# Compression's product in two parts, and the attention gate's projections ahead of the recurrent steps, in a decoder trunk of two layers

## The chip, the cores and the metric

The kernel runs on one core of one Trainium2 chip. The metric is the device time of one execution in microseconds. A core has five engines with a queue each, and each works through its own instructions in the order in which they stand: TensorE (PE, with its weight loads as PEld), VectorE (DVE), ScalarE (ACT), GpSimd (POOL) and SyncE (SP). Engines wait for each other, and for transfers, by semaphores. In this kernel SyncE and ScalarE issue all the transfers.

## What is computed

Two layers over a sequence of 1024 tokens of width 1024. Each layer normalises, projects with one wide matrix, and splits the result among four mixers: attention in three branches, a gated MLP, a convolution module and an RWKV-7 recurrence. Each mixer's output is multiplied by its own gate, an output projection and a residual follow, then a gated per-layer embedding. The parts that matter here:

```python
def nsa_compress(k, pos, w1, w2):
    ch = k.reshape(B, S // CMP_STRIDE, CMP_STRIDE, dk)
    blk = jnp.concatenate([ch[:, :-1], ch[:, 1:]], axis=2) + pos
    flat = blk.reshape(B, -1, CMP_BLOCK * dk)
    return jax.nn.silu(flat @ w1) @ w2          # w1: (2048, 128), once for keys, once for values

# conv module:  x = a * sigmoid(b); causal depthwise convolution of 31 taps; ...
# RWKV-7:
def step(state, inp):
    sa = jnp.einsum('bhvk,bhk->bhv', state, -kk_t)
    state = state * w_t + sa * (kk_t * a_t) + v_t * k_t
    return state, jnp.einsum('bhvk,bhk->bhv', state, r_t)

# layer: mix = concat(y_a * silu(z_a), y_b * silu(z_b), y_c * silu(z_c), y_d * silu(z_d))
```

## The kernel before, in words

The work is cut into four halves: half 0 and half 1 are the two halves of the sequence (512 tokens each) in the first layer, halves 2 and 3 the same in the second. For each half the string in `ORDER` names the steps in the order in which they are written: H norm, F the recurrence's front, R its chain (`rwkv_chain`, which calls `rwkv_solve`), N the attention's front (`nsa_front`), r the recurrent steps (`rwkv_steps`), G the convolution's GLU, a, b, c, d the four gates' projections (`zgate`), s the gated MLP, n the recurrence's norm, A a tile of attention, T the convolution's taps, C its end, O and g the output products of the half before, and so on. That order is a priority, not the final order: the framework's scheduler decides at build time, from priority and its own idea of how long things take, where each engine's instructions stand. On the chip these orders are fixed.

Activations lie with channels on partitions and tokens along the row. Every dense product is made in three passes of 128x512 (`mm3`, L168 to L170: high times high, low part of the activations, low part of the weights). Weights come in granules of 128x512: a load into `ws` (L152), a cast to the high part `wh` on ScalarE (L158), a difference that gives the low part `wl` on GpSimd (L160), and in the first half of each layer a store of the low part to DRAM (L163, `low`), from which the second half loads it (L157). `ws`, `wh` and `wl` have three buffers each. A projection of 128 columns is 24 dense products and two granules.

The recurrence is done in chunks of 64 tokens. Its chain makes, for all chunks and heads, the inverse of a unit triangular matrix: TensorE makes the matrices (L444, L447), VectorE masks them (L465), SyncE stores them to DRAM (`Nd`, L459, L466) and loads them back with one matrix to a partition (L471 into `q`, L476 into `l`). VectorE then solves row by row, 15 rounds of a product and a sum (L484, L486) and 16 more (L506, L508), a long series in which each round needs the one before. The result goes to DRAM from ScalarE's queue (`Xd`, L496), and the steps load it back on SyncE's (`x`, L536). In `rwkv_tri` TensorE's first product with it is L540, VectorE masks that (L543), the second product is L547, and VectorE adds (L550). The steps themselves are L588 to L626 on TensorE with VectorE, ScalarE and GpSimd in between (L596, L601, L608, L621), eight chunks one behind the other. L647 and L648 belong to the norm behind them.

The compression's product (L871) multiplies patches of the keys and values (`im`, made on VectorE at L856) with `nsa_w1`, whose eight parts of 128x512 are loaded on SyncE into the pool `ld` (`load_w1`, L831). The pool has five buffers. So five parts (four of the keys', one of the values') are loaded at the start of `nsa_front`, and the other three when the product itself has let go of a buffer. The product stands at the end of `nsa_front`, behind the key, value and query projections, and is followed by four short steps to the compressed keys and values (L874 to L902).

The convolution's GLU (L679 on VectorE) stands behind two projections; as soon as it is there, VectorE can start on the 31 taps for each of two groups of channels (L691, then 30 of L694, 60 in a half), which have no hurry. A gate's projections end in L658 on ScalarE and L659 on VectorE.

## Time and profile before

| | us |
|---|---|
| median of three runs | 1815.43 |
| lowest and highest of the three | 1801.3, 1817.22 |
| the profiled execution, its own time | 1803.61 |
| its span, first to last instruction | 1801.9 |

| engine | busy us | share of the span | instructions |
|---|---|---|---|
| PE | 1676.2 | 93% | 10068 |
| DVE | 1207.2 | 67% | 3217 |
| ACT | 798.9 | 44% | 1801 |
| POOL | 400.1 | 22% | 327 |

A busy engine is not yet the bound: the share is a mean over stretches with different limits. What to read is which wait ends last in a stretch. In the rows below, a number in brackets behind an instruction is the time in which its engine stood idle before it, with what ended that. The granted clock of TensorE is given as a share of its full level (1.00 is 2.4 GHz, 0.50 is 1.2 GHz); over the whole span it was 0.966.

### The profile page before, as it was taken

How to read it: one execution, taken by the hardware profiler on the slowest of the kernel's cores; microseconds unless marked ns; L12 is line 12 of the kernel's file. 1: busy time of each engine (PE TensorE's matmuls, PEld its weight loads, DVE VectorE, ACT ScalarE, POOL GpSimd, SP SyncE). 2: the span in 40 equal slices, each digit the busy share in tenths (PEclk: the TensorE clock that was granted, in tenths of full speed). 3: DMA queues.
4: the chain of work that ended last, by engine and by line, in shares of the span. 5: the costliest groups of instructions: out<-in, count | busy, mean ns of one | idle time of the engine just before them, and what ended most of it. 6: DMA issues, size and time to landing. Idle time of an engine off the chain costs nothing. (4 is left out here: it accounts for less than half of the span.)

```text
span 1801.9 us, 29197 instructions
## 1 busy us (share of the span) xinstructions
PE 1676.2 (93%) x10068; PEld 1237.6 (69%) x10068; DVE 1207.2 (67%) x3217; ACT 798.9 (44%) x1801; POOL 400.1 (22%) x327
## 2 busy tenths in 40 slices
PE   5997999999999999989988999999999999998998
PEld 4665666767776766666666667666777777766777
DVE  5649887765988647566499961667578885464263
ACT  4432244653234655544322434556333446553443
POOL 3333233000011232233332323000000102323343
PEclk9999998999999999989989999999999999989989
DMA  8466553326844523464574455753475433114554
GB/s 270 135 158 151 163 164 114 108 83 156 226 137 118 164 94 122 154 184 127 148 177 144 127 183 172 235 172 104 124 195 157 120 106 106 42 53 146 170 164 123
DMA packets 361419, 261.19 MB, mean 145 GB/s; under 512 B 84652, under 2 KB 296624, under 8 KB 361272
## 3 DMA queue, kind: packets, MB, share of 16 engines
q1 hardware_dynamic: 318520, 245.17, 46.8%
q10 hardware_dynamic: 42752, 14.16, 3.1%
q8 instruction: 79, 1.29, 0.3%
q14 instruction: 68, 0.56, 0.1%
HBM read 191.50 MB, written 67.77 MB: 144 GB/s over the span
## 5 line engine op out<-in xcount | busy, mean ns | idle before, releaser
L168 PE MATMUL mm<-aT,wh 128*128 128x512 f32 (+1 forms) x1304 | 537.4, 414 | 7.6 <-ACT aT L257 2.8
L169 PE MATMUL mm<-aT,wh 128*128 128x512 f32 (+1 forms) x1304 | 531.0, 408 | 3.3 <-DVE aT L258 3.1
L170 PE MATMUL mm<-aT,wl 128*128 128x512 f32 (+1 forms) x1304 | 529.0, 406 | 0.2 <-POOL wl L160 0.2
L160 POOL TENSOR_TENSOR wl<-ws,wh 128x512 fp32r<-128x512 f32 (+1 forms) x228 | 307.3, 1350 | 697.2 <-ACT wh L158 593.5
L158 ACT CAST wh<-ws 128x512 fp32r<-128x512 f32 (+2 forms) x388 | 237.1, 611 | 477.7 <-PE mm L169 297.4
L168 PEld LDWEIGHTS mm<-aT,wh 128*128 128x128 f32 (+1 forms) x1304 | 249.6, 192 | 68.5 <-issue 6.2
L169 PEld LDWEIGHTS mm<-aT,wh 128*128 128x128 f32 (+1 forms) x1304 | 249.1, 191 | 58.1 <-DVE aT L258 7.4
L170 PEld LDWEIGHTS mm<-aT,wl 128*128 128x128 f32 (+1 forms) x1304 | 249.2, 191 | 51.6 <-issue 3.3
L694 DVE SCALAR_TENSOR_TENSOR cv<-cv,cw,cv 128x512 f32<-128x512 f32 x240 | 198.2, 843 | 2.3
L973 ACT COPY pt<-pt 128x512 f32<-128x512 f32 (+1 forms) x152 | 80.6, 530 | 110.8 <-PE pt L970 110.1
L608 POOL TENSOR_TENSOR q<-SB,gc 128x256 f32<-128x256 f32 x28 | 23.0, 821 | 474.6 <-DVE SB L621 178.7
L1032 ACT ACTIVATE r<-s,sma 128x512 f32<-128x512 f32 (+3 forms) x192 | 105.8, 554 | 46.4 <-DVE sma L1030 42.9
L970 PE MATMUL pt<-cst,r 128*128 128x128 f32 x528 | 103.2, 294 | 9.5 <-DVE r L1037 9.2
L978 PEld LDWEIGHTS pv<-pt,vs 128*64 128x64 f32 x1056 | 56.4, 138 | 58.4 <-ACT pt L973 48.5
L978 PE MATMUL pv<-pt,vs 128*64 128x128 f32 x1056 | 94.4, 291 | 2.2 <-ACT pt L973 1.8
L970 PEld LDWEIGHTS pt<-cst,r 128*128 128x128 f32 x528 | 60.9, 143 | 45.9 <-issue 24.7
L1022 DVE CUSTOM_DVE_ANT_0 s<-s,T 128x256 f32<-128x256 f32 (+1 forms) x144 | 54.0, 378 | 42.8 <-PE s L1003 42.1
L1002 PE MATMUL s<-kv,qs 128*128 128x512 f32 (+2 forms) x192 | 74.3, 389 | 0.8 <-ACT r L1032 0.8
L1037 DVE TENSOR_SCALAR r<-r,sma 128x640 f32<-128x640 f32 (+7 forms) x128 | 67.4, 526 | 1.0
L1003 PE MATMUL s<-kv,qs 128*128 128x512 f32 (+2 forms) x192 | 65.7, 346 | 0.0
L1034 DVE TENSOR_TENSOR sma<-sma 128x1 f32<-128x1 f32 x64 | 14.1, 220 | 71.2 <-ACT r L1032 70.9
L1113 DVE SCALAR_TENSOR_TENSOR ot<-ot,ld 128x512 f32<-128x512 f32 x24 | 25.1, 1049 | 51.3 <-ACT ot L1112 49.4
(328 smaller groups left out, 2652.7 us busy)
## 6 DMA issues: line engine op xcount, KB each, us to landing
ws<-in_w_in_dram SPq DMA_DIRECT2D x232, 256.0 KB, 3.2
wl<-low SPq DMA_DIRECT2D x156, 256.0 KB, 2.9
low<-wl SPq DMA_DIRECT2D x140, 256.0 KB, 2.1
ws<-in_ple_gate_dram SPq DMA_DIRECT2D x64, 256.0 KB, 3.0
ws<-in_w_out_dram SPq DMA_DIRECT2D x60, 256.0 KB, 2.9
ped<-ot ACTq DMA_DIRECT2D x32, 256.0 KB, 3.6
ld<-in_nsa_w_dram SPq DMA_DIRECT2D x32, 256.0 KB, 4.0
ld<-ped SPq DMA_DIRECT2D x32, 256.0 KB, 3.7
```

The costliest lines, as they stand in the source:

```text
L158: nc.scalar.copy(hi[:, :cols], st[:, :cols])
L160: nc.gpsimd.tensor_sub(lo[:, :cols], st[:, :cols], hi[:, :cols].bitcast(F32))
L168: nc.tensor.matmul(out, lh, rh, start=first, stop=False, skip_group_check=shared)
L169: nc.tensor.matmul(out, lh, rl, start=False, stop=False, skip_group_check=shared)
L170: nc.tensor.matmul(out, ll, rh, start=False, stop=last, skip_group_check=shared)
L694: nc.vector.scalar_tensor_tensor(ac, xg[j][:, k:k + TH], cw[:, j * 31 + k:j * 31 + k + 1], ac, op0=OP.mult, op1=OP.add)
L970: nc.tensor.transpose(pt[:, o:o + 128], P[e][:, (b + x - b0) * 128:(b + x - b0) * 128 + 128], self.ident)
L973: nc.scalar.copy(PT[:, :n], pt[:, :n])
L978: nc.tensor.matmul(acc[e], w.VS[hh][:, tt, br], PT[:, o:o + 128], start=False, stop=br == 1 and b + x == i, skip_group_check=True)
L1002: nc.tensor.matmul(p[:, :n], w.QS[hd][:, qs], w.KH[br, hh][:, c0 * 128:c1 * 128], start=True, stop=False)
L1032: nc.scalar.activation(P[:, o:o + wd], p[:, c:c + wd], AF.Exp, bias=ng[:, 0:1], accum_out=den[:, x:x + 1])
L1037: nc.vector.tensor_scalar(P[:, :n], P[:, :n], r, None, op0=OP.mult)
```

## The change

The product is cut in two. `compress_half` makes the keys' half right behind the patches, ahead of the key, value and query projections, into a bank of the pool `pv` instead of `pt`, and at its end issues the three loads that are left. `compress_out` makes the values' half at the old place. In the order of steps, `a` (the attention gate's two projections) moves ahead of `r` in halves 0 and 2, and with that ahead of G, which stays behind `r`. Halves 1 and 3 keep their strings.

```diff
-ORDER = ("XieHFZRNrGaBbscdnAAATCy",
+ORDER = ("XieHFZRNarGBbscdnAAATCy",
          "HAFRNGrbsaAAAAdcniOexTgCy",
-         "HFRNrGabscdniOxeAAgAATyC",
+         "HFRNarGbscdniOxeAAgAATyC",
          "HFRNGraAbsAAnAcdOTxgCy")
@@ nsa_front
         self.w1 = [self.load_w1(x) for x in range(5)]
         im = self.compress_in()
+        ph = self.ps("pv")
+        self.compress_half(ph, im[0], 0)
         VT = self.t2(TH)
...
-        self.compress_out(*im)
+        self.compress_out(ph, *im)
@@
-    def compress_out(self, im, ns, nn):
+    def compress_half(self, ph, im, kv):
+        for g in range(4):
+            w = self.w1[4 * kv + g]
+            for i in range(4):
+                self.nc.tensor.matmul(ph[32 * i:32 * i + 32, kv * 128:kv * 128 + 128], im[kv][:, g * 4 + i],
+                                      w[:, i * 128:i * 128 + 128], start=(g == 0), stop=(g == 3))
+        self.w1 += [self.load_w1(x) for x in range(len(self.w1), 8)]
+
+    def compress_out(self, ph, im, ns, nn):
         nc, h = self.nc, self.h
-        ph = self.ps("pt")
-        for kv in range(2):
-            for g in range(4):
-                x = 4 * kv + g
-                w = self.w1[x] if x < len(self.w1) else self.load_w1(x)
-                for i in range(4):
-                    nc.tensor.matmul(ph[32 * i:32 * i + 32, kv * 128:kv * 128 + 128], im[kv][:, g * 4 + i],
-                                     w[:, i * 128:i * 128 + 128], start=(g == 0), stop=(g == 3))
+        self.compress_half(ph, im, 1)
         part = self.t2(256)
```

(In the call for the first half, `im` is what `compress_in` returned, a triple, so `im[0]` is the list of the two patches.) In the changed file the lines behind `nsa_front` have other numbers: the product is L869, the load of its weights L833, the patches L858.

TensorE in half 0, around the compression's product, before. `mm` are banks of dense products, `ld` the product's weights, `t` its patches; `pt_1246` is the product's bank:

```order
L170 MATMUL mm_1199<-aT_316,wl_1223 128x512
L871 MATMUL pt_1246<-ld_981,t_224_1036 32x128 x4
L871 MATMUL pt_1246<-ld_983,t_224_1036 32x128 x4
L871 MATMUL pt_1246<-ld_985,t_224_1036 32x128 x4
L871 MATMUL pt_1246<-ld_987,t_224_1036 32x128 x4
L871 MATMUL pt_1246<-ld_989,t_225_1042 32x128 x4
...
L871 MATMUL pt_1246<-ld_1267,t_225_1042 32x128 x4
...
L871 MATMUL pt_1246<-ld_1273,t_225_1042 32x128 x4
...
L871 MATMUL pt_1246<-ld_1279,t_225_1042 32x128 x4
```

The same place in the change; the keys' half stands a hundred rows earlier:

```order
L170 MATMUL mm_1222<-aT_316,wl_1246 128x512
L869 MATMUL pv_1048<-ld_989,t_225_1042 32x128 x4
L869 MATMUL pv_1048<-ld_1065,t_225_1042 32x128 x4
L869 MATMUL pv_1048<-ld_1067,t_225_1042 32x128 x4
L869 MATMUL pv_1048<-ld_1069,t_225_1042 32x128 x4
L168 MATMUL mm_1311<-aT_281,wh_1314 128x512
```

Before, the last three parts of the values' half stood spread among dense products, 28, 9 and 10 of them apart; now the four parts stand together, and the dense products behind them are those of the attention gate (`mm_1311`, `mm_1355`) and then two and a half of the GLU's four projections, 111 in all up to L540, where 130 stood before (the GLU's 96, then the gate's).

VectorE in half 0, near the end of the solve, before. `q` and `l` belong to the solve, `cv` to the convolution:

```order
L508 TENSOR_REDUCE q_207_924<-q_206_893 128x8
L897 CAST kcl_1297<-kcl_1297 64x31
L694 SCALAR_TENSOR_TENSOR cv_3357<-cv_1792,cw_99,cv_3357 128x512
L506 TENSOR_TENSOR q_206_893<-l_205_884,q_207_924 128x232
L694 SCALAR_TENSOR_TENSOR cv_3357<-cv_1792,cw_99,cv_3357 128x512
L508 TENSOR_REDUCE q_207_924<-q_206_893 128x8
L694 SCALAR_TENSOR_TENSOR cv_3357<-cv_1792,cw_99,cv_3357 128x512
L506 TENSOR_TENSOR q_206_893<-l_205_884,q_207_924 128x240
L694 SCALAR_TENSOR_TENSOR cv_3357<-cv_1792,cw_99,cv_3357 128x512
L508 TENSOR_REDUCE q_207_924<-q_206_893 128x8
```

The same place in the change; `y_1352` and `y_1396` are the attention gate:

```order
L506 TENSOR_TENSOR q_206_893<-l_205_884,q_207_924 128x208
L659 SCALAR_TENSOR_TENSOR y_1352<-y_1352,mm_1311 128x512
L508 TENSOR_REDUCE q_207_924<-q_206_893 128x8
L659 SCALAR_TENSOR_TENSOR y_1396<-y_1396,mm_1355 128x512
L506 TENSOR_TENSOR q_206_893<-l_205_884,q_207_924 128x216
L508 TENSOR_REDUCE q_207_924<-q_206_893 128x8
...
L508 TENSOR_REDUCE q_207_924<-q_206_893 128x8
L679 SCALAR_TENSOR_TENSOR cv_1880<-t_388_1883,mm_1926 128x512
L683 COPY xhalo_2054<-cv_1880 128x30
L691 TENSOR_SCALAR cv_3357<-cv_1880,cw_99,par_92 128x512
L694 SCALAR_TENSOR_TENSOR cv_3357<-cv_1880,cw_99,cv_3357 128x512 x4
L543 TENSOR_TENSOR q_296_1406<-rp_1401,cst 64x128 x2
```

The GLU and six taps that stood between the last rounds of the solve are behind them now, four of the taps ahead of the first L543 and the others among the steps; two rows of the gate have come in.

SyncE in half 0, in the change, where the three loads stand now (before, they stood some 30 rows later, between stores of `low` parts):

```order
L833 DMA ld_1065<-in_nsa_w_dram 128x4x128
L833 DMA ld_1067<-in_nsa_w_dram 128x4x128
L466 DMA Nd_83<-q_194_848 64x256
L833 DMA ld_1069<-in_nsa_w_dram 128x4x128
L276 DMA ab_3476<-in_xT_dram 128x512
L163 DMA low_1149<-wl_1146 128x512
```

They have come between the stores that feed the solve (L466).

## Rows read from the trace of the kernel before

**Rows 1.** Waits of PE over the span: total us, times, longest us.

```profile
PE pt L871 <- DMA ld<-in_nsa_w_dram: 16.5, 9, 4.5
PE rp L540 <- DMA x<-Xd: 7.2, 4, 4.4
```

**Rows 2.** Busy us (instructions) in stretches: PE, PEld, DVE, ACT, POOL, clock, DMA.

```profile
132.60:180.70 48.10, 37.74 (x212) 28.52 (x211) 46.07 (x93) 11.74 (x24) 15.40 (x11) 0.91 0.62 155
180.70:293.00 112.30, 106.24 (x819) 78.82 (x820) 98.12 (x255) 42.75 (x102) 39.43 (x34) 0.98 0.57 164
443.20:480.00 36.80, 34.70 (x208) 26.32 (x207) 35.33 (x77) 11.80 (x24) 1.59 (x2) 1.00 0.96 230
899.70:947.40 47.70, 39.52 (x212) 29.61 (x211) 45.67 (x92) 11.81 (x24) 17.22 (x12) 0.89 0.72 182
947.40:1066.40 119.00, 110.49 (x825) 81.08 (x825) 105.05 (x261) 41.33 (x101) 38.80 (x33) 0.94 0.45 133
```

**Rows 3.** Timeline of PE: start us, us, instruction, count [idle before, what ended it].

```profile
147.53 0.39 PE L169 MATMUL mm<-aT,wh 128*128 128x512 f32 x1
...
148.22 0.39 PE L169 MATMUL mm<-aT,wh 128*128 128x512 f32 x1
153.09 0.66 PE L871 MATMUL pt<-ld,t 128*32 128x128 f32 x8 [4.49 <-DMA ld<-in_nsa_w_dram]
...
180.76 0.69 PE L540 MATMUL rp<-x,at 64*64 64x64 f32 x8 [4.42 <-DMA x<-Xd]
...
951.78 0.69 PE L547 MATMUL rp<-x,q 64*64 64x64 f32 x8 [2.55 <-DVE q L543]
...
1365.17 0.45 PE L540 MATMUL rp<-x,at 64*64 64x64 f32 x8 [0.32 <-DMA x<-Xd]
```

**Rows 4.** Groups: half 0's solve (DVE, POOL), half 2's L694, the span (next two), half 0's steps.

```profile
L694 DVE SCALAR_TENSOR_TENSOR cv<-cv,cw,cv 128x512 f32<-128x512 f32 x6 | 5.4, 900 | 0.0
L679 DVE SCALAR_TENSOR_TENSOR cv<-t,mm 128x512 f32<-128x512 f32 x1 | 0.7, 691 | 0.0
L691 DVE TENSOR_SCALAR cv<-cv,cw,par 128x512 f32<-128x512 f32 x1 | 0.5, 544 | 0.0
L160 POOL TENSOR_TENSOR wl<-ws,wh 128x512 fp32r<-128x512 f32 x9 | 12.3, 1361 | 26.4 <-ACT wh L158 20.9 <-DMA Xd<-q 5.4
...
L694 DVE SCALAR_TENSOR_TENSOR cv<-cv,cw,cv 128x512 f32<-128x512 f32 x6 | 6.2, 1035 | 0.0
...
L659 DVE SCALAR_TENSOR_TENSOR y<-y,mm 128x512 f32<-128x512 f32 x32 | 21.9, 683 | 2.4 <-ACT y L658 1.9
L938 DVE TENSOR_TENSOR pt<-pt,TC 128x256 f32<-128x256 f32 x16 | 6.9, 431 | 3.6 <-PE pt L933 3.3
...
L694 DVE SCALAR_TENSOR_TENSOR cv<-cv,cw,cv 128x512 f32<-128x512 f32 x42 | 36.0, 871 | 0.5
```

**Rows 5.** Timeline of DVE and POOL in the solves of halves 0 and 2.

```profile
160.63 1.34 POOL L160 TENSOR_TENSOR wl<-ws,wh 128x512 fp32r<-128x512 f32 x1 [4.67 <-ACT wh L158]
160.74 1.70 DVE L506 TENSOR_TENSOR q<-l,q 128x232 f32<-128x232 f32 x1
168.24 0.64 DVE L506 TENSOR_TENSOR q<-l,q 128x248 f32<-128x248 f32 x1
...
943.58 5.75 DVE L694 SCALAR_TENSOR_TENSOR cv<-cv,cw,cv 128x512 f32<-128x512 f32 x7
```

**Rows 6.** Timeline of SP's queue: issues of transfers, half 0.

```profile
148.85 0.53 SPq L831 DMA_DIRECT2D ld<-in_nsa_w_dram  x1
...
176.31 0.34 SPq L163 DMA_DIRECT2D low<-wl  x1
...
177.30 0.91 SPq L536 DMA_DIRECT2D x<-Xd  x2
```

**Rows 7.** Busy us in two stretches behind a wait, with the granted clock.

```profile
178.80:185.60 6.80, 4.83 (x24) 3.46 (x25) 6.65 (x13) 0.62 (x1) 1.27 (x1) 0.50 0.52 158
...
1339.30:1346.10 6.80, 6.32 (x26) 4.03 (x26) 5.82 (x16) 1.67 (x6) 0.64 (x1) 0.50 0.69 200
```

## The prediction, made before the changed kernel ran

> **What bounds the kernel now.** I read the waits first, then stretches of busy time, then single rows. TensorE is busy for 93% of the span, and every half of every layer has two places where it stands still around the same work. The first is the compression's product (L871), which waits for its own weights: 16.5 us in nine waits over the four halves [rows 1]. The second comes 40 us later: the first product of the recurrent steps (L540), which waits for the solved blocks `x` to come back from DRAM, 7.2 us in four waits [rows 1].
>
> The point to see is that these two stand one behind the other in TensorE's fixed order, and that the second is not TensorE's doing. `x` is made by a chain on VectorE (L484 to L508), then stored on ScalarE's queue (L496), then loaded on SyncE's (L536). Between the first half of the product and L540 VectorE is busy 46.07 of 48.1 us in half 0 and 45.67 of 47.7 in half 2 [rows 2]: it sets the time of L540. In half 0 TensorE waits 4.49 us at L871 and then still 4.42 us at L540; in half 3 L540 comes just in time, 0.32 us late [rows 3]. So time saved at L871 mostly lengthens the wait at L540, and the change is worth what it does to the chain on VectorE and to the steps behind it.
>
> **The change part by part.** I work each half out as the shift of the place where TensorE's order and the amount of work ahead of it are equal again. Counted in the two orders, the number of dense products (L168 to L170) ahead of the end of the steps (L647) is the same before and after in halves 0, 1 and 2, and 23 larger after in half 3, equal again behind it. One dense product takes 0.23 us (147.53 to 148.22 in three) [rows 3].
>
> *The loads.* Now 5 to 7 are issued as soon as the first half of the product is done, 20 us ahead of need, instead of behind it. The waits of 16.5 us go. On SyncE's queue the three loads now stand ahead of a store that feeds the solve (L466); they wait for TensorE's first-half product, whose patches (L856) VectorE makes ahead of the rows that the store carries, so I cost this at 0 (bound: their own time at the queue, one of them 0.53 us [rows 6], 1.6 us a half).
>
> *Half 0, the chain.* In its last ten rounds VectorE now also runs the GLU and taps: six taps of 5.4 us, L679 0.7 and L691 0.5, 6.6 us together [rows 4], and a copy of 30 columns. From start to start it is 6.1 us, since neighbours overlap by some 0.1. After the change two gate rows (L659, 0.68 each [rows 4]) and one small copy stand there: 1.5 us. GpSimd makes a low part (L160) for each granule of weights, nine in this stretch at 1.36 us [rows 4], and one that ran at 160.63 made a round of the chain take 1.70 us at 160.74, where a later round took 0.64 [rows 5]. TensorE no longer stops, so one or two more of these fall into the chain: I take 1 us. The chain ends 6.1 - 1.5 - 1 = 3.6 us sooner. The stores behind it take as long as now; but the load of `x` at 177.30 stood behind a store of 176.31 that waited for GpSimd [rows 6], and in the new order those ahead of it are old by then: 1 us more (0 to 2). L540 comes 4.6 us sooner. But ahead of it stand 111 dense products instead of 130 (counted from the last query projection), so 19 come later: 4.3 us. Net -0.3.
>
> The Trainium skill (SBUF — State Buffer, "Who interferes with whom") says that a VectorE operation with two SBUF inputs and a GpSimd operation that reads SBUF exclude each other for the whole of the one that came first. The row of 160.74 agrees: 1.1 us of delay against a GpSimd operation of 1.34 us. By that rule two more of them could cost 2.7 us where I take 1, and the sum would be 3 to 4 us higher over halves 0 and 2.
>
> *Half 0, the steps.* What left the chain has to be done later: by the orders 4 taps instead of 19 are done at the first L543, 57 instead of 60 at the end (L648): 12 taps more in the steps at 0.87 us by the mean of their group [rows 4], 10 us, where VectorE is busy 98.12 of 112.3 us [rows 2]. The stretch itself grows by 4.3 us, so 14.2 + 4.3 us of idle time stand against 10. It fits, at a price: more products of the steps will find VectorE at a tap. I take 1.3 us (0 to 6). Half 0: +1 (-1 to +6).
>
> *Half 2* has the same chain. Out go six taps (6.2 us [rows 4]) and as many others: 7.4 us, 6.9 from start to start. In come the two L659 and the first softmax rows of an attention tile (L938 0.43 [rows 4], and five more that I estimate at 0.3 each from it): 3 us with the two L659; GpSimd 1. Chain -2.9, load of `x` -0.6, L540 3.5 us sooner; 12 dense products (2.7 us) come later, 1.3 us of attention products earlier. At present the second product of the steps (L547) waits 2.55 us [rows 3], because L543 sits behind seven taps of 5.75 us on VectorE at 943.58 [rows 5]; after the change six taps stand there and are done before `x` lands: -2.5. Taps in the steps, 8 more, VectorE busy 105.05 of 119 [rows 2]: +1. Half 2: -3.5 (-7 to +2).
>
> *Halves 1 and 3* keep their step order, but the product moves there too. Half 1 has little to give: the dense products ahead of L540 are equal in number, and VectorE is busy 35.33 of 36.8 us [rows 2]: -0.5 (-1.6 to +1). Half 3 saves 3.7 us of waits and the 3.2 us that a stretch at the low clock costs behind them (6.32 us busy at 0.50 from 1339.30 [rows 7]). But since the GLU now comes sooner, VectorE's order puts 11 taps instead of 7, a second L679 and three attention rows into the chain: 4.9 us, of which 1.7 fill time in which it is idle today. L540, now only just in time, comes 3.2 us later with TensorE waiting some 6 us; 13 dense products and attention products (4.5 us) are done ahead of it instead of behind. A wait of 4.42 us at L540 was followed by the low clock in half 0 (178.80, 4.83 us busy at 0.50 [rows 7]), so I charge 2 us: +0.7 (-4 to +5).
>
> **Sum.** +1 - 3.5 - 0.5 + 0.7 = -2.3 us against the profiled execution's 1803.61 us, which is at the low end of the three runs (1801.3 to 1817.22); the same difference taken from their median 1815.43 gives 1813.
>
> **The rivals.**
> *The saved waits stay saved.* If the chain follows the freer TensorE, as it would if its rounds wait more for weights and GpSimd than I see, then 16.5 us of waits, 2.5 us at L547 and three stretches at the low clock of about 3.2 us go: 28.6 us, 1787. For it: half 1, whose wait at L540 is small. Against it: VectorE's 96% ahead of L540 in halves 0 and 2. It decides from the point where L540's wait stays under 2 us in halves 0 and 2. Chance 0.12.
> *VectorE becomes the bound in the steps.* It ends on the other side. Some 20 taps move into two stretches where VectorE is 87 to 88% busy; at 0.87 us they are 17 us, and if none of its idle time takes them, because that lies in short pieces behind TensorE's products, the halves lose 17 - 4.6 - 3.5 = 9 us, with half 3 at its upper bound 5 more: +14, 1829; with two more GpSimd operations in each of the two chains that hold VectorE for their whole 1.36 us, 4 us more, 1833. Against it: in half 0 TensorE waited for VectorE little in the steps as they are (its busy time is 106.24 of 112.3 us [rows 2]). It decides where idle time at L547, L588 and L647 grows by more than 6 us a half. Chance 0.15.
> *The change does nothing* that can be seen: that is the forecast's neighbour and lies in its range.
>
> **How the numbers follow.** Forecast, the wait moves from L871 to L540: 0.73. Its own bounds are the sums of those above, -14 to +14 us: 1802 to 1829. The three runs differ by 16 us, so I lower the floor to 1796, which leaves the first rival's end out, and put the top at 1828. A measurement of this kernel tells about 1% (18 us) from no change. Faster by over 1% is the first rival's whole price or most of it, 0.12; slower by over 1% needs the second rival's upper end, 0.07; the rest, 0.81, lies within.
>
> **What would show it.** Right: no wait of the compression's product for `ld`; in half 0 a wait at L540 of 10 to 14 us, in half 2 of 9 to 13, in half 3 of some 6; the last L508 about 3.6 us sooner after its first L484 in half 0; VectorE over 90% busy in the steps of halves 0 and 2. Wrong: waits at L540 as short as now with a shorter span (first rival); or L647 more than 5 us later than now in half 0 (second rival).

## The result, and the profile after

| | before | after |
|---|---|---|
| median of 22 runs each, us | 1810.93 | 1820.99 |
| ratio, with its 95% interval | | 1.0056 (1.0040 to 1.0071) |
| the profiled execution: its own time, span, us | 1803.61, 1801.9 | 1817.79, 1816.1 |

The change makes the kernel 10 us slower. The forecast was 2.3 us faster; the time lies in the range that was given, the sign was wrong. The two profiled executions differ by 14.2 us, 4 more than the medians. Lines behind the changed functions moved on: the product is L869 now (L871 before), its chain L877 to L905, the loads L833.

The waits of TensorE over the span (in total, times, longest), after the change:

```profile
PE mm L168 <- DVE y L659: 14.5, 5, 5.2
...
PE pt L888 <- DVE cth L885: 9.7, 4, 3.2
...
PE c L599 <- DVE q L596: 5.4, 5, 1.5
...
PE rp L547 <- DVE q L543: 2.8, 4, 1.0
PE rp L540 <- DMA x<-Xd: 2.7, 4, 0.8
```

The 16.5 us of waits for weights [rows 1] are gone, as forecast. They did not go to L540, whose wait fell from 7.2 us [rows 1] to 2.7. They came back at two places that hardly waited before: at L888, the step of the compression's chain that needs VectorE's L885 (in the kernel before these are L885 and L882), and at a dense product (L168) that finds both of its PSUM banks held, because VectorE has not yet done the gate's L659. The two in the kernel before:

```profile
PE mm L168 <- DVE y L659: 0.4, 1, 0.4
...
PE pt L885 <- DVE cth L882: 0.4, 1, 0.4
```

Where the first of each falls after the change (timeline of TensorE, with the idle time before an instruction):

```profile
140.57 0.31 PE L888 MATMUL pt<-cth,w 128*64 128x31 f32 x4 [3.18 <-DVE cth L885]
...
157.98 0.79 PE L168 MATMUL mm<-aT,wh 128*128 128x512 f32 x1 [5.20 <-DVE y L659]
...
176.11 0.39 PE L540 MATMUL rp<-x,at 64*64 64x64 f32 x6 [0.83 <-DMA x<-Xd]
```

These are half 0's. Over the whole program TensorE stands idle for 1816.1 - 1686.9 = 129.2 us, where it was 1801.9 - 1676.2 = 125.7. So idle time makes only 3.5 of the 14.2 us; for the other 10.7 TensorE is busy longer with the same 10068 instructions, at a mean granted clock of 0.963 instead of 0.966:

```profile
PE 1686.9 (93%) x10068; PEld 1242.1 (68%) x10068; DVE 1200.4 (66%) x3217; ACT 799.0 (44%) x1801; POOL 394.0 (22%) x327
```

Where the time was lost shows when the same places are set beside each other (start times from the two timelines of TensorE, us). At L540 the work ahead is not the same: 19 dense products fewer stand ahead of it in half 0 and 12 fewer in half 2.

| place | before | after | shift |
|---|---|---|---|
| half 0: L540, first product of the steps | 180.8 | 176.1 | -4.7 |
| half 0: L647, end of the steps | 292.9 | 296.6 | +3.7 |
| half 0: L732, end of the convolution | 311.1 | 321.9 | +10.9 |
| half 1: transposition of the values (L812, now L814) | 434.7 | 447.5 | +12.8 |
| half 1: L540 | 480.0 | 498.0 | +18.0 |
| half 1: L647 | 599.8 | 621.0 | +21.2 |
| half 2: L540 | 947.4 | 965.6 | +18.2 |
| half 2: L647 | 1063.6 | 1084.1 | +20.5 |
| half 3: the recurrence's front (its first L428) | 1251.5 | 1268.5 | +17.0 |
| half 3: first transposition of an output block (L1133, now L1136) | 1634.0 | 1651.8 | +17.8 |

All of it arises in halves 0 and 1; halves 2 and 3 give 3 to 4 us back, and the work behind the last row 3.6 more, to 14.2 at the end. The busy times of the stretches of half 0 (solve, steps, convolution's end), and half 2's steps (us, then PE, PEld, DVE, ACT, POOL with counts, granted clock, DMA share, GB/s); the first row is the convolution's end before the change, the others are after it:

```profile
292.90:311.10 18.20, 15.38 (x86) 10.88 (x84) 12.94 (x49) 8.52 (x22) 1.98 (x2) 0.74 0.24 77
```

```profile
131.00:176.10 45.10, 35.34 (x172) 26.78 (x170) 35.37 (x81) 11.28 (x23) 14.94 (x12) 0.89 0.74 173
...
176.10:296.60 120.50, 113.03 (x840) 84.33 (x841) 105.77 (x268) 42.93 (x105) 41.47 (x35) 0.96 0.50 148
...
296.60:321.90 25.30, 20.16 (x97) 14.03 (x96) 18.49 (x57) 10.49 (x25) 1.99 (x2) 0.67 0.14 46
...
965.60:1084.10 118.50, 110.15 (x825) 81.50 (x826) 104.17 (x265) 41.42 (x96) 39.43 (x34) 0.96 0.47 139
```

In the solve VectorE is now busy 35.37 of 45.1 us, where it was busy 46.07 of 48.1 [rows 2]. Most of the work that left it is done in the steps, where VectorE is busy 105.77 us instead of 98.12 [rows 2]; the rest is done at the other end: from L647 to L732 it is busy 18.49 us instead of 12.94, and that stretch, in which TensorE has little else, takes 25.3 us instead of 18.2. VectorE's timeline there, first after the change, then before:

```profile
302.81 0.73 DVE L694 SCALAR_TENSOR_TENSOR cv<-cv,cw,cv 128x512 f32<-128x512 f32 x1
...
303.82 0.74 DVE L694 SCALAR_TENSOR_TENSOR cv<-cv,cw,cv 128x512 f32<-128x512 f32 x1
...
307.57 0.69 DVE L708 TENSOR_TENSOR cv<-cv,c 128x512 f32<-128x512 f32 x1 [1.34 <-PE c L704]
```

```profile
298.16 0.68 DVE L708 TENSOR_TENSOR cv<-cv,c 128x512 f32<-128x512 f32 x1
```

Six taps (L694) of half 0 run behind the start of L647 after the change, none before. L708, which needs the last of them, comes 11.0 us behind L647 (296.55) where it came 5.3 us behind it (292.89).

### The profile page after: what moved, and what is told of

Same layout as the page of the kernel before. It is cut to its first block, busy times and chain, and to the rows that moved or that the text cites. A ratio compares the mean times of both kernels' runs of the same rounds, so it can differ in the third digit from the quotient of the medians.

```text
span 1816.1 us, 29189 instructions
## 1 busy us (share of the span) xinstructions
PE 1686.9 (93%) x10068; PEld 1242.1 (68%) x10068; DVE 1200.4 (66%) x3217; ACT 799.0 (44%) x1801; POOL 394.0 (22%) x327
## 5 line engine op out<-in xcount | busy, mean ns | idle before, releaser
L168 PE MATMUL mm<-aT,wh 128*128 128x512 f32 (+1 forms) x1304 | 538.4, 415 | 22.6 <-DVE y L659 14.5
L160 POOL TENSOR_TENSOR wl<-ws,wh 128x512 fp32r<-128x512 f32 (+1 forms) x228 | 302.9, 1331 | 671.7 <-ACT wh L158 549.8
L168 PEld LDWEIGHTS mm<-aT,wh 128*128 128x128 f32 (+1 forms) x1304 | 250.2, 192 | 87.9 <-DVE y L659 16.5
L694 DVE SCALAR_TENSOR_TENSOR cv<-cv,cw,cv 128x512 f32<-128x512 f32 x240 | 187.5, 795 | 2.3
L1035 ACT ACTIVATE r<-s,sma 128x512 f32<-128x512 f32 (+3 forms) x192 | 105.8, 555 | 66.5 <-DVE sma L1033 63.2
L1025 DVE CUSTOM_DVE_ANT_0 s<-s,T 128x256 f32<-128x256 f32 (+1 forms) x144 | 54.1, 376 | 38.1 <-PE s L1006 37.3
L1116 DVE SCALAR_TENSOR_TENSOR ot<-ot,ld 128x512 f32<-128x512 f32 x24 | 26.1, 1088 | 51.2 <-ACT ot L1115 45.7
```

What stands on the lines that cost most here:

```text
L160: nc.gpsimd.tensor_sub(lo[:, :cols], st[:, :cols], hi[:, :cols].bitcast(F32))
L168: nc.tensor.matmul(out, lh, rh, start=first, stop=False, skip_group_check=shared)
L694: nc.vector.scalar_tensor_tensor(ac, xg[j][:, k:k + TH], cw[:, j * 31 + k:j * 31 + k + 1], ac, op0=OP.mult, op1=OP.add)
L1035: nc.scalar.activation(P[:, o:o + wd], p[:, c:c + wd], AF.Exp, bias=ng[:, 0:1], accum_out=den[:, x:x + 1])
```

## The experiments

Theories at the start: (1) the loss is shared, the split costs by its chain at L888 in half 1 and the moved gate costs in half 0; (2) the moved gate alone costs; (3) the split alone costs. All runs, each against runs of the kernel before on the same chip (whose medians were 1809.2 to 1811.8 us; its mean granted clock 0.961 to 0.963):

| run | median us | ratio (95%) | mean clock |
|---|---|---|---|
| after the change | 1820.99 | 1.0056 (1.0040 to 1.0071) | 0.963 |
| e1_split | 1816.29 | 1.0030 (1.0010 to 1.0051) | 0.964 |
| e2_order | 1838.97 | 1.0157 (1.0128 to 1.0187) | 0.953 |
| e3_a0 | 1827.38 | 1.0096 (1.0071 to 1.0121) | 0.959 |
| e4_a2 | 1810.19 | 1.0007 (0.9990 to 1.0024) | 0.966 |
| e5_noload | 1814.14 | 1.0030 (1.0011 to 1.0049) | 0.964 |
| e6_g0 | 1809.25 | 1.0000 (0.9982 to 1.0018) | 0.967 |
| e7_taps_after | 1815.24 | 1.0033 (1.0010 to 1.0056) | 0.968 |
| e8_taps_a2 | 1817.85 | 1.0046 (1.0026 to 1.0066) | 0.965 |
| e9_open | 1827.34 | 1.0102 (1.0072 to 1.0131) | 0.957 |
| e10_casts | 1824.83 | 1.0081 (1.0061 to 1.0102) | 0.963 |
| e11_casts_before | 1824.09 | 1.0068 (1.0041 to 1.0096) | 0.958 |
| e12_casts_a2 | 1817.90 | 1.0052 (1.0032 to 1.0072) | 0.964 |
| e13_g0_whole | 1816.42 | 1.0038 (1.0017 to 1.0060) | 0.961 |
| e14_a2_whole | 1813.01 | 1.0014 (0.9994 to 1.0035) | 0.963 |
| e15_late | 1833.91 | 1.0134 (1.0102 to 1.0166) | 0.953 |
| e16_late_g0 | 1835.20 | 1.0150 (1.0118 to 1.0182) | 0.949 |
| e17_pool | 1818.12 | 1.0027 (1.0008 to 1.0046) | 0.966 |
| e18_pool_g0 | 1805.26 | 0.9982 (0.9961 to 1.0004) | 0.969 |

**The parts of the change, one by one.** The split with the order of before:

```diff
-ORDER = ("XieHFZRNarGBbscdnAAATCy", ..., "HFRNarGbscdniOxeAAgAATyC", ...
+ORDER = ("XieHFZRNrGaBbscdnAAATCy", ..., "HFRNrGabscdniOxeAAgAATyC", ...
```

> The split alone: the product in two parts with its loads in between, and the gate's projections of halves 0 and 2 left where they were. Set beside each other, the two traces differ by +3.7 us at the end of the steps (L647) of half 0, +18 at the start of the steps of half 1, +21 at their end, and then by nearly nothing more (+18 at the start of half 3, +14 at the end). Theory 1 (the parts share the loss: the short chain behind the second part of the product, which in all four halves now waits for VectorE at L888 (9.7 us in four waits), costs in half 1, the moved gate in half 0): +3 to +8 us on the kernel before, a wait of 2 to 3 us at L888 in each half. Theory 2 (the moved gate alone costs): 0 to -5 us, since the 16.5 us of waits for weights go. Theory 3 (the split alone costs): +9 to +12 us.

It costs 0.3%, 5 us. Its waits:

```profile
PE rp L540 <- DMA x<-Xd: 11.7, 5, 5.7
PE pt L888 <- DVE cth L885: 8.9, 4, 3.6
...
PE mm L168 <- DVE y L659: 4.7, 2, 3.3
```

So 16.5 us of waits for weights are exchanged for 4.5 more at L540, 8.9 at L888, 4.7 behind L659. The new order with the product in one piece (the two strings of the change in the kernel before):

> The move of the gate alone, in halves 0 and 2, with the product in one piece where it was and its waits for weights. Theory 1 (shared): +3 to +8 us, with the wait of a dense product for a bank that the gate's L659 holds (14.5 us in five waits after the change) seen in halves 0 and 2. Theory 2 (the moved gate alone costs): +9 to +12 us. Theory 3 (the split alone costs): 0, within 3 us.

It costs 28 us, more than any theory gave: the parts are not independent. A large part of it goes with the clock: a mean of 0.953 instead of 0.962, with levels of 1.00 and 0.50 only, puts 9.4% of the time at the lower level instead of 7.6%, some 173 us instead of 137. If TensorE does half as much in that time, this is 18 of the 28 us (an estimate from these means). The split with the gate ahead of the steps in half 0 only, and in half 2 only (one string of the change taken back each time):

> The split with the gate moved in half 0 only. After the change the shift grew to +18 us up to the steps of half 1 and no further in half 2, so theory 1 and theory 2 expect nearly the whole loss here: +8 to +12 us on the kernel before. Theory 3: the same as with the split alone, within 3 us of it.

> The split with the gate moved in half 2 only, where the shift fell by 1 to 3 us after the change. Theory 1: like the split alone, or 1 to 3 us better, so 0 to +6 us on the kernel before. Theory 2: -1 to -8 us. Theory 3: +7 to +12 us.

In half 0 the move takes the split from 1.0030 to 1.0096, in half 2 to 1.0007. That has the signs of theory 1: the split costs some, half 0's move costs more, half 2's move gives about 4 us back (the intervals of e1 and e4 overlap). Its size for half 0 was too small: e3 is 17 us slower than the kernel before, and theory 1 gave 8 to 12.

**What the waits for weights were worth.** The kernel before, where the last three parts of the product take weights that are already there:

```diff
-                w = self.w1[x] if x < len(self.w1) else self.load_w1(x)
+                w = self.w1[x] if x < len(self.w1) else self.w1[x - 4]
```

> The kernel before, its order and its product in one piece, with loads 5 to 7 of the compression's weights left out: the last three parts of the product use the weights of loads 1 to 3 again (their result is another). So the product waits for nothing of its own and moves nowhere. Theory 1 (a wait saved there comes back at the next place that waits for VectorE): the waits of 16.5 us at L871 go, but waits at the short chain behind the product (L885) and at L540 take most of it; -5 to +2 us on the kernel before. Rival (the waits are worth their time and the low clock behind them): -16 to -28 us.

Nothing: without those waits, and with the product where it was, the kernel is 0.3% slower, a little more than even theory 1 gave (-5 to +2 us). The waits in its profile:

```profile
PE rp L540 <- DMA x<-Xd: 10.2, 5, 4.0
PE pt L877 <- ACT t L874: 8.9, 4, 4.1
```

L877 is the product's next step in that kernel, and hardly waited before. The saved waits come back at the next places that depend on ScalarE and VectorE.

**Why half 0's move costs.** The suspicion from the profile was VectorE's late taps. Twenty-four of half 0's taps are left out (21 us of VectorE), in the changed kernel and in that of e4:

```diff
-            for k in range(1, 31):
+            for k in range(1, 31 if self.l or self.h else 19):
```

> The changed kernel with 24 of the 62 convolution taps of half 0 left out (21 us of VectorE by their mean of 0.87 us), to be set against the next run, where the same taps are left out and the gate stands behind the steps in half 0. With all taps the two differ by 10.8 us (1820.99 against 1810.19). Theory 1 (the moved gate makes the GLU and so the taps late, and TensorE pays for VectorE's late work in the steps of half 0 and behind them): this run is within 3 us of the next one. Rival (the place of the dense products costs, whatever VectorE has to do): it stays 8 to 13 us slower than the next one.

> The split with the gate moved in half 2 only, with the same 24 taps of half 0 left out. Both theories: somewhat faster than with the taps (1810.19), by 0 to 8 us, since in half 0 VectorE is busy 9 tenths of the steps. It is the base for the run before it.

The difference of 10.8 us between the two is gone (-2.6), as theory 1 said, but the base did not behave: e8, with 21 us less to do on VectorE than e4, is slower by 7.7 us, and that is more than half of what closes the gap. The pair supports the theory and does not prove it. What their profiles do show: with no tap left behind L647, the stretch from L647 to L732 of half 0 takes 17.5 us in e7 and 17.6 in e8, as short as before. The clean test leaves all work in and moves one letter, the GLU (`G`), ahead of the gate and the steps in half 0:

```diff
-ORDER = ("XieHFZRNarGBbscdnAAATCy",
+ORDER = ("XieHFZRNGraBbscdnAAATCy",
```

> The split, the gate moved in half 2, and in half 0 the convolution's GLU and the gate both ahead of the steps, the GLU first. So even more dense products leave the steps of half 0 than in the changed kernel, but the GLU comes early, and the taps with it. In the profiles so far the stretch from the end of the steps (L647) to the end of the convolution (L732) of half 0 is 5 to 8 us longer than before wherever the gate stands ahead of the steps with all taps, and within 1 us of before in all others. Theory 1 (late taps): that stretch stays within 2 us of before, and the run is within 5 us of 1810. Rival (dense products missing in the steps and behind them): the stretch is again 5 us longer or more, and the run above 1818.

This kernel differs from the changed one in that string alone, and is level with the kernel before: 10 us less by the ratios, 11.7 by the medians. The stretch from L647 to L732 of half 0, in e3 (GLU late) and in e6 (GLU first), with the columns as above:

```profile
298.60:324.70 26.10, 21.18 (x97) 15.47 (x96) 18.41 (x57) 10.55 (x25) 1.99 (x2) 0.61 0.15 47
```

```profile
301.20:320.60 19.40, 15.82 (x83) 11.86 (x81) 12.76 (x49) 8.91 (x23) 1.98 (x2) 0.70 0.29 92
```

With the GLU first no tap is left behind L647, VectorE is busy 12.76 us instead of 18.41, and the stretch takes 19.4 us, near the 18.2 of before. The profiles of all runs but e11 agree here: it takes 23.2 to 26.1 us in the six profiles with six or seven late taps (after, e2, e3, e9, e10, e17) and 17.5 to 21.8 in the others. So late taps cost the changed kernel some 6 us at the convolution's end. A second difference stands beside it: half 1's solve begins (first L484 on VectorE) 1.3 us behind that half's transposition of the values in e6, 2.1 us in the kernel before, and 5.9 in the changed kernel, 5.7 in e3, 5.2 in e2. But this is not shown to come from the taps: the solve begins 5.5 us behind in e7 and in e8 too, where no tap of half 0 is late, and 5.1 in e15, whose gate was not moved. Nor do the two make up the difference of the medians: in e6 the steps of half 0 end 4.7 us later and half 1's solve is 3.7 us longer than in the changed kernel, and the two profiled spans differ by 4.8 us. That half 0's loss comes with the late GLU is shown by the times; through the taps, some 6 us of it are.

With the product in one piece, the same two moves apart:

> The kernel before, product in one piece, with the GLU and the gate both ahead of the steps in half 0, the GLU first. The changed order without the split cost 28 us. Theory 1 (late taps behind the gate in half 0): with the GLU first nothing of it is left in half 0, within 5 us of the kernel before. Rival (dense products taken out of the steps of half 0 cost, with the product in one piece above all): +10 us or more.

> The kernel before, product in one piece, with the gate ahead of the steps in half 2 only. With the split the same move measured 6 us less than the split alone (1810.19 against 1816.29). Theory 1 (half 0 makes the 28 us of the changed order without the split): within 5 us of the kernel before. Rival (half 2 makes a part of it): +6 us or more.

With the GLU first, half 0's move costs 7 us in one piece, a little more than theory 1 gave; half 2's costs nothing that can be told. The two together make some 11 us of the 28 of e2. The other 17 may come with the late GLU, or with the lower clock of e2; these runs do not separate the two. Nor do these two profiles show where a loss arises: 4.9 (e13) and 4.7 us (e14) are there at the first L428 of half 0, up to which every engine runs the same instructions in the same order as before. TensorE's last stop ahead of it, at L389, is 2.57 us long in both and 2.56 before; then, from 56.0 to 60.5 us, the granted clock is 0.50 in both and 1.00 in the kernel before.

**Why the split costs.** Four tries at the wait at L888. First, the chain opened: the product's second part and L885 ahead of the queries' projections, L888 behind them:

```diff
         self.VS[h] = VS
+        th = self.compress_out(ph, *im)
         self.QS = []
...
-        self.compress_out(ph, *im)
+        self.compress_end(th, *im[1:])
```

> The changed kernel with the chain behind the product opened: the product's second part and its step on VectorE (L885) stand between the keys' and the queries' projections, and what reads them (L888 and behind) stays behind the queries' projections, so 48 dense products lie between. In the changed kernel L888 waits 9.7 us in four waits, and a low-clock stretch of 3.4 or 6.8 us begins behind each of three of them. Theory 1 (a cost of its own): the four waits go, -9 to -15 us on the changed kernel, so 1806 to 1812. Rival (they come back at L540 or at the dense product that waits for a bank held by L659): within 4 us of the changed kernel, 1817 to 1825. The loads now have some 14 us, 11 of them dense products, instead of 25 to land: if they are late, a wait for `ld` shows.

The wait at L888 goes and comes back one link further, at the transposition of the compressed values (10.6 us in four waits, longest 4.1); 6 us slower than the changed kernel, where the theory gave 9 to 15 us faster. Next, a wait in ScalarE's queue: the second query cast waits for VectorE's low part of the first, and the chain's step L884 stands behind it. In the changed kernel:

```profile
138.15 0.59 ACT L825 ACTIVATE qs<-mm 64x512 fp32r<-64x512 f32 x1 [3.50 <-DVE qs L826]
138.77 0.22 ACT L884 ACTIVATE cth<-pt 128x62 f32<-128x62 f32 x1
```

Both casts of a pair are issued ahead of both low parts, in the changed kernel, in the kernel before, and in e4:

```diff
+            for e in range(2):
+                nc.scalar.mul(QS[e][0:64], qp[64 * e:64 * e + 64], 0.125)
+            for e in range(2):
+                nc.vector.scalar_tensor_tensor(QS[e][64:128], qp[64 * e:64 * e + 64], 0.125, ...
```

> The changed kernel with one wait taken out of ScalarE's queue: for each pair of query heads both casts (L825) are issued ahead of both low parts (L826), so that the second cast no longer waits for VectorE's low part of the first; in the changed kernel ScalarE stands 3.50 us at 138.15 and 2.54 us at 460.13 there, with the step L884 of the compression's chain queued behind it. Theory 1 (the waits at L888 come from VectorE through that place in ScalarE's queue): the four waits of 9.7 us at L888 fall below 4 us, idle time does not come back in that stretch, and the time falls by 4 to 12 us on the changed kernel: 1809 to 1817. Rival (TensorE is tied to VectorE's solve in that stretch at every link, and the wait only moves on, as in the run with the chain opened): within 4 us of the changed kernel or slower.

> The same reordering of casts and low parts in the kernel before, as its control. There the chain behind the product stands later, behind the product's own waits for weights, and ScalarE has no step of it queued in that place. Theory 1: within 4 us of the kernel before. Rival: it gains as much as in the changed kernel, which would make it a thing of its own.

> The split, the gate moved in half 2 only, and casts ahead of low parts. Without the casts it measured 1810.19. Theory 1: 4 to 12 us less, 1798 to 1806, and so faster than the kernel before by 0.2 to 0.6 per cent. Rival: within 4 us of 1810.

All three are slower than without it, by 4, 13 and 8 us. That theory falls. In e10 the step on ScalarE did come sooner, and L888 waited all the same, for VectorE's own step in its own queue (ScalarE, VectorE, TensorE):

```profile
137.39 0.22 ACT L884 ACTIVATE cth<-pt 128x62 f32<-128x62 f32 x1 [0.72 <-PE pt L880]
```

```profile
141.69 0.40 DVE L484 TENSOR_TENSOR q<-q,q 128x144 f32<-128x144 f32 x1
142.12 0.22 DVE L885 SCALAR_TENSOR_TENSOR cth<-cth,pt 128x62 f32<-128x62 f32 x1
```

```profile
142.40 0.31 PE L888 MATMUL pt<-cth,w 128*64 128x31 f32 x4 [3.11 <-DVE cth L885]
```

L885 is ready 4.5 us before it runs; it stands between two rounds of the solve. Third, the second part and its chain put behind the GLU, near the place in VectorE's order that they had before the change; in e1 and in e6:

```diff
-        self.compress_out(ph, *im)
+        self.late = ph, *im
...
                     elif step == "G":
                         self.conv_glu()
+                        self.compress_out(*self.late)
```

> The split alone, as in the run of the split, but with the product's second part and its chain issued behind the convolution's GLU in all four halves. The early loads and the first part stay. Theory 1 (the split costs because the chain's step on VectorE, L885, now stands 30 instructions earlier in VectorE's order, in the first rounds of the solve, where TensorE waits for it): the four waits at L888 (8.9 us) fall below 3 us, and the run comes back to the kernel before or below it: -8 to +1 us on it. Rival (the early first part and its loads cost by themselves, or the saved wait returns at L540 in any place): +4 to +8 us, as the split alone.

> The run with the GLU and the gate ahead of the steps in half 0 (1809.25, level with the kernel before), with the product's second part and its chain behind the GLU. Theory 1: 4 to 8 us less, 1801 to 1805. Rival: within 4 us of 1809.

24 and 26 us slower than the kernel before; by the estimate made for e2, their clocks of 0.953 and 0.949 against 0.963 hold some 19 and 26 us of that. In e15 L888 waits more, not less:

```profile
PE pt L888 <- DVE cth L885: 16.7, 4, 7.2
PE mm L168 <- ACT t L678: 13.3, 3, 6.0
```

Fourth, the step L885 taken off VectorE, on top of the casts, in the changed kernel and in e6:

```diff
-        nc.vector.scalar_tensor_tensor(th[:, :, :nn], th[:, :, :nn], 1.0, pv, op0=OP.add, op1=OP.mult)
+        cp = self.t([128, 2, 32], "ctc", bufs=1)
+        nc.scalar.copy(cp[:, :, :nn], pv)
+        nc.gpsimd.tensor_mul(th[:, :, :nn], th[:, :, :nn], cp[:, :, :nn])
+        nc.gpsimd.tensor_add(th[:, :, :nn], th[:, :, :nn], cp[:, :, :nn])
```

> The changed kernel with casts ahead of low parts (as the run e10_casts, 1824.83) and with the chain's step L885 taken off VectorE: ScalarE copies the sums out of PSUM and GpSimd multiplies and adds them in two small operations, so no link of the chain up to L888 is VectorE's. Theory 1 (the wait at L888 has a price of its own, and was VectorE's queue): the 8.2 us at L888 fall below 3 us, and the time falls by 6 us or more on the run with the casts, below 1819. Rival (TensorE's idle time in the solve is set by VectorE, and comes back wherever TensorE next meets it: L540, the bank that L659 holds, L547): the wait at L888 falls, TensorE's waits for VectorE and for `x` grow by as much, and the time stays within 4 us of 1825 or above.

> The split with the GLU and the gate ahead of the steps in half 0 and the gate ahead of them in half 2 (1809.25), with casts ahead of low parts and the step L885 on GpSimd. Theory 1: 6 us or more below it, 1803 or less, and faster than the kernel before. Rival: within 5 us of 1809 or slower.

The waits in e17:

```profile
PE mm L168 <- DVE y L659: 17.7, 6, 5.3
...
PE rp L540 <- DMA x<-Xd: 6.0, 4, 3.2
PE rp L647 <- DVE y L648: 5.4, 2, 2.7
PE pt L906 <- ACT vct L904: 5.4, 3, 2.3
```

The 8.2 us at the chain's product are gone, and the bank held by L659 costs 3.7 us more than in e10 (14.0), the compressed values' transposition 5.4: the waits moved on, as the rival said. Yet the time fell by 6.7 us on e10, as theory 1 said. Both were half right. e18, at 0.9982, is the fastest kernel of all, 6.6 us below the kernel before in the medians; its interval still reaches 1.0004, so it is not shown to beat it. Against e6 it gains 4.0 us, where theory 1 wanted 6 and the rival allowed 5: here the rival's size came.

**What the split does to VectorE.** From the first L484 to the end of the last L508 in each half (us, from VectorE's timeline):

| | half 0 | half 1 | half 2 | half 3 |
|---|---|---|---|---|
| before | 38.7 | 33.3 | 38.1 | 34.6 |
| split alone (e1) | 40.1 | 35.8 | 40.2 | 37.2 |
| after the change | 33.1 | 34.0 | 34.7 | 37.7 |
| e6 | 41.8 | 37.7 | 34.8 | 37.4 |
| e18 | 41.0 | 35.7 | 34.1 | 36.4 |
| order alone (e2) | 32.1 | 31.5 | 32.9 | 34.6 |

With the split alone the solve gets 1.4 to 2.6 us longer in every half. In halves 0, 1 and 3 three, three and four more taps stand in it; in half 2 there are as many taps as before (seven), and rows of the attention's softmax have come in. Half 3's groups of VectorE, before and in e1 (count, busy us, mean ns):

```profile
L694 DVE SCALAR_TENSOR_TENSOR cv<-cv,cw,cv 128x512 f32<-128x512 f32 x8 | 5.9, 742 | 0.0
```

```profile
L694 DVE SCALAR_TENSOR_TENSOR cv<-cv,cw,cv 128x512 f32<-128x512 f32 x12 | 8.9, 741 | 0.0
```

With the product elsewhere, the scheduler puts a second GLU row and four more taps into the solve; why it does so is not shown. The last row of the table shows the limit of this reading: e2 has the shortest solves of all and is among the slowest. It has late taps too (six of half 0's behind L647), and beside them its lower clock (0.953) is a rival cause of its time.

## Why the prediction was wrong, and where it was right

- *L871 waits for weights, 16.5 us, and they go.* Right. But the sum gave the place of their return as L540, "so time saved at L871 mostly lengthens the wait at L540". **This step failed.** L540's wait fell to 2.7 us; the return was at L888 and behind L659, 24.2 us together. The prediction had looked for what is late next at the end of VectorE's chain only, and not at TensorE's other needs of VectorE on the way: the chain behind the product and the banks of the gate's projections. That a wait saved there is worth little was right, and e5 shows it.
- *Half 0, the chain: 3.6 us sooner, L540 4.6 us sooner, 19 dense products later, net -0.3.* Right in the whole, and in part by luck: the chain is 5.6 us shorter (38.7 to 33.1), but the way from its end to L540 got 1.0 us longer (10.9 to 11.9) where 1 us less was forecast, so L540 is 4.7 us sooner with the 19 fewer products ahead of it, 0 to -0.4 net. Another term had the wrong sign: one or two more GpSimd operations were expected in the chain, and L160 ran 7 times there, where it had run 9 times [rows 4]. The rule of the Trainium skill (SBUF — State Buffer, "Who interferes with whom") would have charged more for them; the rows agree with the rule itself (in the changed kernel a round of 36 columns that takes 0.22 us in half 1 took 1.23 at 133.88 us, beside a GpSimd operation that began at 133.75), but there were fewer chances for it. GpSimd's group in that solve:

```profile
L160 POOL TENSOR_TENSOR wl<-ws,wh 128x512 fp32r<-128x512 f32 x7 | 9.5, 1354 | 19.0 <-ACT wh L158 11.2 <-ACT kch L897 6.4 <-DMA Xd<-q 1.4
```

- *Half 0, the steps: 12 more taps fit into 18.5 us of idle time, +1.3 (0 to 6).* The size was a little low, +4.0 at L647 (3.7 and the 0.3 of the chain). **The second step that failed is the sentence under it:** that where the number of dense products ahead is equal, nothing is owed. The orders showed 57 taps of 60 done at L648, and the last three, with what stands around them, were priced at nothing. Six taps run behind the start of L647 and hold up L708 by 5.7 us where TensorE has little dense work left: the stretch to L732 takes 25.3 us instead of 18.2, and the shift grows by 7.2. This term alone is larger than the whole forecast. The rival "VectorE becomes the bound in the steps" had the right engine and the right cause, late taps; its place, the steps themselves, and its price of 9 us in halves 0 and 2 together, were not: half 2, whose string has output products (`O`, `g`) behind its steps where half 0's has none, lost nothing.
- *Half 1: -0.5 (-1.6 to +1).* Wrong: the shift grows by 8.4 us, from 12.8 at its values to 21.2 at the end of its steps. 3.8 of it is the later start of its solve, which the sum did not hold and whose cause stays open (e7 and e8 have it without late taps); 3.2 more arise in its steps, and a wait of 2.35 us at L888 lies in its solve. In e1, without the moved gate, half 1's solve is 2.5 us longer, filled in the way shown for half 3.
- *Half 2: chain -2.9, L547's wait gone, -3.5 (-7 to +2).* Right: the chain is 3.4 us shorter, L547 waits at most 1.0 us in the whole program, and the shift falls by 4 us from half 2's start to half 3's. e4 against e1 has 6 us.
- *Half 3: chain 3.2 us longer, +0.7 (-4 to +5).* The chain is 3.1 us longer, and the shift at the first output block is 0.8 more than at half 3's start. That the sum came out is luck: L540's wait of 6 us did not come (none is longer than 0.8), and L540 is shifted by 18.2 us (1365.2 to 1383.4), not 3.2 more than the start of the solve (18.4).
- *The loads on SyncE's queue, at 0.* Not contradicted by e1, e4 and e6, which have them: half 1's solve begins no later behind the projections than before (1.3 to 2.2 us against 2.1). In the changed kernel it does (5.9), and there they are not excluded.
- *The signs.* "A wait at L540 of 10 to 14 us in half 0" (0.83) and "VectorE over 90% busy in the steps" (105.77 of 120.5 us, 88%, and 104.17 of 118.5) did not come; the last L508 "3.6 us sooner" did, by 5.6.

What stays open: why e5 is slower than the kernel before although nothing but waits and loads were taken from it; why less work on VectorE (e8) and one wait less on ScalarE (e10 to e12) cost 4 to 13 us; why half 1's solve begins late; and which of L885 and the longer solves makes the split's 5 us. For e8 and e12 the profiles show the place: the steps of half 0 (L540 to L647) take 121.4 and 124.4 us where they take 113.2 in e4. TensorE runs nearly the same number of instructions there (817 and 811 against 810) and is busy with them for 111.6 and 114.9 us against 105.8, at a granted clock of 0.90 and 0.88 against 0.95. So most of what these two lose lies in time at the lower clock in one stretch; why the clock fell there is not shown.

## What to carry to other kernels

When a wait is taken from an engine in a stretch in which another engine sets the pace, list every instruction of the first that needs the second on the way (small chains, banks that are held), not just the last one: the saved time stops at the first of them. And follow filler work that is pushed out of a busy stretch to where it is finished; if it ends behind the last piece of work that could cover it, it costs about its length (here six taps, some 6 us), and the order of its source (here the GLU ahead of a gate, 10 us) can be worth more than the wait. Parts of such a change should be tried one by one, since here they cost +5, -4 and +12 us. And a local difference between two profiles is not yet its cause: a run in which the supposed cause is absent (here e7 and e8, without late taps) shows whether the difference goes with it.

## What was not expected of the hardware

The two profiles suggest that the clock takes part: 0.966 before, 0.963 after. Over all runs that isn't so: the mean granted clock is 0.963 after the change and 0.961 to 0.963 before it. But within one kernel the clock goes with the time: in 23 runs of the kernel before, spans and clocks have a correlation of -0.90, and their spans differ by 13 us. One profiled execution can stand 7 us (the kernel before) or 13 us (e1, 1803.1) beside its kernel's median, so shifts like those in the table above were believed only where several kernels showed them. The slowest kernels are those whose clock fell most, 0.949 to 0.953 in e2, e15 and e16. That the clock can fall with the same work and the same stops is seen in e13 and e14, in the first 61 us.
